# Preparing the output weights' block sums during the projections: another ring of buffers, loads 5 to 12 slots ahead, sums issued one at a time

## The chip, the cores and the metric

The kernel runs on one core of a Trainium2 chip. A core has a matrix engine (PE; its weight loads are listed as PEld), a vector engine (DVE), a scalar engine (ACT), a general-purpose engine (POOL, also called GpSimd) and a queue that issues DMA transfers (SP). Each works through its own list of instructions in order, and waits where an instruction needs what another engine or a transfer has not yet delivered. The metric is the device time of one execution in microseconds (us); lower is better.

## The reference

One layer of an encoder over two sequences (256 and 2048 rows of width 1024), in float32:

```python
h = rms_norm(x, g_pre)
proj = h @ w_in                                  # 1024 -> 3072
q, k, v, z_a, u_f, z_f = jnp.split(proj, ...)
y_a = neighbourhood_attention(q, k, v, rpb)      # 8 heads, windows of 8 x 16
y_f = fourier_mix(u_f, w_fourier, b_fourier)     # 2-D FFT by groups, then a matrix
mixed = jnp.concatenate([rms_norm(y_a, g_na) * jax.nn.silu(z_a),
                         rms_norm(y_f, g_f) * jax.nn.silu(z_f)], axis=-1)
return x + rms_norm(mixed @ w_out, g_post)
```

What matters here: `w_out` (in the code `wo`, the half of it that multiplies the Fourier branch) is used near the end of the kernel, in products of Strassen's form. Such products need differences of blocks of the weights. They depend on the weights alone, so the kernel makes them early, in a stage whose own work is the projections, and stores them in memory (`wtD`) for later.

## The kernel before

**Products.** A float32 operand is split into a high and a low part (`wa`: ACT copies the high part, L573 or L576; DVE subtracts to get the low part, L574 or L577), and each product is three matmuls (L164, L165, L166).

**The stage.** The projections to z, k and q of the long sequence run in the loop `for i in range(16)`, with an inner loop `for j in range(7)`: the seven products of a Strassen step. One pair (i, j) is a *slot*, numbered 7*i + j. A slot is 12 matmuls of 128x512 into one PSUM tile. Slots 0 to 55 work on the first half of the rows, and the change lies in these. PSUM tiles come from `mmt`, a rotation of five (three of tag `a`, two of tag `t`): the product of slot n + 5 writes the tile of slot n, so slot n must have been read out by then. Slots with j = 0 are read by ACT (L1022), all others by DVE (L935 into the output tile `f`, L1020 into a running sum).

**Order.** The order of every engine's list is that of the code: whatever is called in slot n is listed there. Engines run as far ahead or behind as their waits let them. In each slot the code calls, among others: `w_load` (weights two steps ahead) and `w_sums` (their block sums one step ahead, on POOL, L559), `a_split` (the split of the next step's weights, ACT then DVE), in some slots `n_load`, `n_scale` (DVE, L427), `n_diff` (POOL, L435, and a store `n_put`, L431) for the second half's rows, and at i = 5 `t_mask` (POOL, L612).

**The sums.** The block differences are made in four pieces x = 0 to 3, each of 128 x 1024 numbers: `wt_load` (two DMAs, L748), `wt_scale` (two ACT instructions, L754), four subtractions of 128 x 256 (L759, each depends on others of the piece), and `wt_store` (two DMAs, L765). The table `WT` gives the slot in which each step is called; within a slot these calls come after those named above, except `t_mask`. A piece lies in a tile of the pool `st` with tag `f`, three buffers in rotation. The two output tiles `o` of each step i come from the same three.

## Time and profile before

| what | value |
|---|---|
| time, median of 3 runs (lowest to highest) | 960.85 us (957.23 to 961.78) |
| the profiled execution's own time / its span | 957.96 us / 956.2 us |
| busy: PE / DVE / ACT / POOL | 944.2 / 735.0 / 505.3 / 448.2 us |
| slots 0 to 55 (first half of the projections) | 156.2 to 313.4 us of the span |

The span is the time between the first and the last instruction. PE is listed as busy for 99% of it; time that PE loses shows as gaps in its list or as a lower granted clock. In rows of the timeline a number in brackets is how long the engine sat idle before the instruction, and behind the arrow is what ended the idle time. Times of rows are counted from the start of the span.

### The profile page before, as it was taken

To read this page: it belongs to the slowest core of one execution; us is meant where nothing else is said; L and a number is where in the kernel's file an instruction comes from. 1 tells how busy PE (TensorE), PEld (TensorE's weight loads), DVE (VectorE), ACT (ScalarE), POOL (GpSimd) and SP (SyncE) were. 2 spreads that over 40 slices of the span, in tenths; PEclk is the share of its full clock that TensorE was granted. 3 is DMA by queue.
4 is the path that set the end of the run, shared out by engine and by line. 5 is a ranking of instruction groups with operands and counts; after the bars stand their busy time and mean duration, and the time that the engine had idled before them with its cause. 6 is when DMAs were issued, how large, how long until landed. Compare 5 with 4: busy or idle time off the path is not lost.

```text
span 956.2 us, 16788 instructions
## 1 busy us (share of the span) xinstructions
PE 944.2 (99%) x5595; PEld 785.2 (82%) x5595; DVE 735.0 (77%) x1355; ACT 505.3 (53%) x1085; POOL 448.2 (47%) x429
## 2 busy tenths in 40 slices
PE   9999999999899999999999999999999999999996
PEld 7889988888788888888888869877888888888885
DVE  6758987786887685598877467777688888859977
ACT  6836676423333642124344266677786676744443
POOL 4100002465770302376555236467599698624444
PEclk9999999999999999999999999999999999999999
DMA  9899697558686995489989898798998989979996
GB/s 357 298 383 335 244 341 276 174 198 323 244 330 245 357 349 192 158 310 366 301 308 365 280 341 268 216 289 265 308 282 274 279 278 305 280 262 326 318 319 218
DMA packets 148486, 276.36 MB, mean 289 GB/s; under 512 B 13126, under 2 KB 85544, under 8 KB 145648
## 3 DMA queue, kind: packets, MB, share of 16 engines
q1 hardware_dynamic: 148048, 274.88, 84.4%
q8 instruction: 45, 0.74, 0.3%
q10 hardware_dynamic: 288, 0.40, 0.1%
q14 instruction: 41, 0.34, 0.1%
q0 software_dynamic: 64, 0.02, 0.0%
HBM read 183.47 MB, written 98.90 MB: 295 GB/s over the span
## 4 chain that ended last, share of the span: by engine, by line
PE 83%; DMA 6%; DVE 5%; issue 3%; POOL 2%; ACT 1%; SPq 0%; DVEq 0%; ACTq 0%; POOLq 0%
PE mm L165 16%; PE mm L164 16%; PE mm L166 16%; PE pv L1639 6%; PE ptb L1623 6%; PE po L1550 6%; PE s L1272 4%; PE px L1706 3%; DMA yr<-yD 3%; PE pz L1706 2%; DVE of L1987 1%; DVE of L1953 1%; DMA f<-wo 1%; POOL nx L435 1%; DMA yo<-xt 1%
## 5 line engine op out<-in xcount | busy, mean ns | idle before, releaser
L164 PE MATMUL mm<-xh,wa 128*128 128x512 f32 x448 | 175.1, 391 | 2.6 <-DVE f L935 2.6
L165 PE MATMUL mm<-xl,wa 128*128 128x512 f32 x448 | 175.0, 391 | 0.0
L166 PE MATMUL mm<-xh,wa 128*128 128x512 f32 x448 | 174.9, 391 | 0.0
L559 POOL TENSOR_TENSOR ws<-wr 128x512 f32<-128x512 f32 x16 | 23.5, 1470 | 212.4 <-DMA wr<-wz 206.6
L1306 POOL TENSOR_SCALAR w<-w,m 128x465 f32<-128x465 f32 (+9 forms) x136 | 86.8, 651 | 40.3 <-DVE m L1303 21.0
L164 PEld LDWEIGHTS mm<-xh,wa 128*128 128x128 f32 x448 | 84.5, 189 | 21.2 <-issue 3.4
L166 PEld LDWEIGHTS mm<-xh,wa 128*128 128x128 f32 x448 | 84.5, 189 | 17.6
L165 PEld LDWEIGHTS mm<-xl,wa 128*128 128x128 f32 x448 | 84.4, 188 | 17.4
L574 DVE TENSOR_TENSOR wa<-wr,wa 128x512 fp32r<-128x512 f32 x60 | 73.0, 1225 | 24.1 <-ACT wa L573 24.0
L1550 PE MATMUL po<-wk,yh 128*128 128x512 f32 x280 | 86.7, 391 | 0.0
L1299 ACT ACTIVATE w<-w,m 128x465 f32<-128x465 f32 (+9 forms) x136 | 78.6, 582 | 13.9 <-DVE m L1294 13.7
L1294 DVE CUSTOM_DVE_ANT_1 w<-s,tb 128x465 f32<-128x465 f32 (+8 forms) x124 | 61.2, 531 | 10.8 <-PE s L1272 9.0
L1988 POOL TENSOR_TENSOR xt<-of,xt 128x512 f32<-128x512 f32 x34 | 43.2, 1294 | 51.9 <-issue 30.3
L612 POOL TENSOR_TENSOR mt<-mt,rmask 128x880 f32<-128x880 f32 (+2 forms) x24 | 50.3, 2111 | 32.5 <-DVE mt L608 20.4
L164 PE MATMUL mm<-vh,xh 128*128 128x512 f32 x168 | 65.4, 389 | 0.0
L165 PE MATMUL mm<-vl,xh 128*128 128x512 f32 x168 | 65.4, 389 | 0.0
L166 PE MATMUL mm<-vh,xl 128*128 128x512 f32 x168 | 65.4, 389 | 0.0
L935 DVE TENSOR_TENSOR f<-u,mm 128x512 f32<-128x512 f32 x64 | 43.5, 680 | 24.4 <-PE mm L166 17.5
L1550 PEld LDWEIGHTS po<-wk,yh 128*128 128x128 f32 x280 | 52.2, 188 | 10.9 <-issue 0.4
L1623 PE MATMUL ptb<-ident,w 128*120 128x128 f32 (+8 forms) x422 | 58.9, 277 | 0.0
L1639 PEld LDWEIGHTS pv<-pt,v 120*64 120x64 f32 (+9 forms) x880 | 47.4, 136 | 12.4 <-issue 7.3
L1623 PEld LDWEIGHTS ptb<-ident,w 128*120 128x120 f32 (+8 forms) x422 | 47.5, 140 | 12.1 <-issue 5.5
(326 smaller groups left out, 2458.9 us busy)
## 6 DMA issues: line engine op xcount, KB each, us to landing
wr<-wz SPq DMA_DIRECT2D x48, 512.0 KB
vl<-sD SPq DMA_DIRECT2D x20, 512.0 KB
xm<-xm SPq DMA_DIRECT2D x9, 1024.0 KB
oD<-ofs SPq DMA_DIRECT2D x18, 512.0 KB
of<-oD SPq DMA_DIRECT2D x18, 512.0 KB
xt<-xn SPq DMA_DIRECT2D x18, 512.0 KB
yo<-xt SPq DMA_DIRECT2D x35, 256.0 KB
yr<-yD SPq DMA_DIRECT2D x34, 256.0 KB
```

The source lines that it names most:

```text
L164: nc.tensor.matmul(out, lh, rh, start=first, stop=False)
L165: nc.tensor.matmul(out, lh, rl, start=False, stop=False)
L166: nc.tensor.matmul(out, ll, rh, start=False, stop=last)
L574: nc.vector.tensor_tensor(out=o[:, 1], in0=src, in1=o[:, 0].bitcast(F32), op=ALU.subtract)
L612: nc.gpsimd.tensor_tensor(out=o, in0=i, in1=rmask[:, m0:m0 + n].unsqueeze(2).to_broadcast([128, n, 80]), op=ALU.add)
L1294: nc.vector.tensor_tensor_reduce(out=rows(g["w"][b][:, h, :n], w), in0=rows(g["s"][2 * b + h][:, :nr * sw(w)], sw(w))[:, :, :w], in1=tv, s ...
L1299: nc.scalar.activation(w, w, AF.Exp, bias=m[:, h:h + 1], scale=-1.0, accum_out=m[:, 2 + h:3 + h])
L1306: nc.gpsimd.tensor_scalar(w, w, m[:, 4 + h:5 + h], 1.0, ALU.mult, ALU.mult)
L1550: nc.tensor.matmul(p, (d["l"] if x == 2 else d["h"])[:, c], w(n, int(x == 1), c), start=j == 0, stop=j == 11)
L1623: nc.tensor.transpose(ptb[h][:nk, j * 128:j * 128 + 128], g["w"][b][:, h, c0:c0 + nk], ident)
L1639: nc.tensor.matmul(p[hs, b], g["v"][:nk, v, hs], g["pt"][b][:nk, h, j * 128:j * 128 + 128], start=j == 0, stop=j == len(ch) - 1)
L1706: nc.tensor.matmul(p, y[:, c], b, start=first and c == i == 0, stop=c == 1 and i == 2, skip_group_check=not first)
```

## The change

The four pieces get tiles of the pool `hp` with tag `vw`, also a rotation of three buffers and of the same size. That rotation serves the row scales that `n_scale` reads (`iv`, called at slot 6, read until slot 27), and, from slot 54 on, the weights of the next stage (`vh`). The four subtractions of a piece are called one by one, each with a slot and an engine of its own. Of the 16, DVE had 8 and now has 2; POOL had 8 and now has 14. Loads stand 5 to 12 slots ahead of the scaling that reads them (before: 2 to 4).

```diff
     def wt_load(x):
         j, c = divmod(x, 2)
-        t = wot[x] = st.tile([128, 2, 2, 256], F32, tag="f", name="f", bufs=3)
+        t = wot[x] = hp.tile([128, 2, 2, 256], F32, tag="vw", name="wt", bufs=3)
...
-    def wt_sums(x, e):
+    def wt_sum(x, n, e):
         (a1, a2), (b1, b2) = [[wot[x][:, y, n] for n in range(2)] for y in range(2)]
-        for o, p, q in ((a1, a2, a1), (a2, b2, a2), (b2, b2, a1), (b1, b1, b2)):
-            e.tensor_tensor(out=o, in0=p, in1=q, op=ALU.subtract)
+        o, p, q = ((a1, a2, a1), (a2, b2, a2), (b2, b2, a1), (b1, b1, b2))[n]
+        e.tensor_tensor(out=o, in0=p, in1=q, op=ALU.subtract)
...
-    WT = ((15, wt_load, 0), (19, wt_scale, 0), (19, wt_sums, 0, nc.gpsimd), (20, wt_store, 0), (24, wt_load, 1),
-          (26, wt_scale, 1), (26, wt_sums, 1, nc.gpsimd), (27, wt_store, 1), (30, wt_load, 2), (33, wt_scale, 2),
-          (33, wt_sums, 2, nc.vector), (39, wt_store, 2), (47, wt_load, 3), (50, wt_scale, 3),
-          (51, wt_sums, 3, nc.vector), (51, wt_store, 3))
+    WT = ((9, wt_load, 0), (21, wt_scale, 0), (24, wt_sum, 0, 0, nc.gpsimd), (24, wt_sum, 0, 1, nc.gpsimd),
+          (24, wt_load, 1), (26, wt_sum, 0, 2, nc.gpsimd), (26, wt_sum, 0, 3, nc.gpsimd), (28, wt_store, 0),
+          (35, wt_scale, 1), (36, wt_sum, 1, 0, nc.vector), (36, wt_load, 2), (37, wt_sum, 1, 1, nc.gpsimd),
...
```

The rest of the new table: piece 1's other sums on POOL at slot 38, its store at 40; piece 2 loaded at 36, scaled at 41, summed at 42 (DVE), 43, 45 and 45, stored at 47; piece 3 loaded at 38, scaled at 47, summed at 48, 48, 49 and 50, stored at 51. Lines behind the table have numbers higher by 4 after the change (L935 becomes L939).

What this does to the lists, at three places. First ACT, slots 26 to 35. Here `wa` is the split of the next step's weights, `f` with itself as input (L940, L944) the SiLU of an output tile, `u` the reading of a product with j = 0. Before:

```order
L754 ACTIVATE f<-f,gmix 128x512 x2
L940 ACTIVATE f<-f 128x1024
L573 CAST wa<-wr 128x512
L940 ACTIVATE f<-f 128x1024
L573 CAST wa<-wr 128x512
L1022 COPY u_2317<-mm 128x512
L573 CAST wa<-wr 128x512
L573 CAST wa<-ws 128x512 x2
L573 CAST wa<-wr 128x512 x2
L754 ACTIVATE f<-f,gmix 128x512 x2
L573 CAST wa<-wr 128x512
```

After:

```order
L944 ACTIVATE f<-f 128x1024
L573 CAST wa<-wr 128x512
L944 ACTIVATE f<-f 128x1024
L573 CAST wa<-wr 128x512
L1026 COPY u_2309<-mm 128x512
L573 CAST wa<-wr 128x512
L573 CAST wa<-ws 128x512 x2
L573 CAST wa<-wr 128x512 x3
L576 ACTIVATE wa<-wr 128x512
L754 ACTIVATE wt<-wt,gmix 128x512 x2
```

The scalings of pieces 1 and 2 (slots 26 and 33) are gone from ahead of the SiLU and of the splits; piece 1's now stands at slot 35.

Second SP, the loads and stores of slots 24 to 36 (`xD<-nx` are the stores `n_put`, `wr<-wz` the weights two steps ahead, `mt<-tr` a table for `t_mask`). Before:

```order
L258 DMA wr<-wz 128x1024 x2
L748 DMA f<-wo 128x2x256 x2
L210 DMA zD<-f 128x1024
L765 DMA wtD<-f 256x1x256 x2
L210 DMA zD<-f 128x1024
L431 DMA xD<-nx 128x1024 x5
L748 DMA f<-wo 128x2x256 x2
L258 DMA wr<-wz 128x1024 x2
L431 DMA xD<-nx 128x1024 x2
```

After:

```order
L258 DMA wr<-wz 128x1024 x2
L748 DMA wt<-wo 128x2x256 x2
L210 DMA zD<-f 128x1024 x2
L431 DMA xD<-nx 128x1024 x3
L765 DMA wtD<-wt 256x1x256 x2
L431 DMA xD<-nx 128x1024 x2
L258 DMA wr<-wz 128x1024 x2
L431 DMA xD<-nx 128x1024 x2
L947 DMA kD<-f 128x1024 x2
L602 DMA mt<-tr 128x1200
L748 DMA wt<-wo 128x2x256 x2
```

Piece 1 is loaded in the same place, its store is no longer between the two stores of z, and the load of piece 2 has moved behind all stores `n_put` and behind the load of `mt`.

Third POOL, slots 28 to 40. Before:

```order
L435 TENSOR_TENSOR nx<-nx 128x1024 x4
L559 TENSOR_TENSOR ws<-wr 128x512
L559 TENSOR_TENSOR ws<-ws,wr 128x512
L559 TENSOR_TENSOR wr<-wr 128x512
L559 TENSOR_TENSOR wr<-wr,ws 128x512
L612 TENSOR_TENSOR mt<-mt,rmask 128x880
```

After:

```order
L435 TENSOR_TENSOR nx<-nx 128x1024 x4
L559 TENSOR_TENSOR ws<-wr 128x512
L559 TENSOR_TENSOR ws<-ws,wr 128x512
L559 TENSOR_TENSOR wr<-wr 128x512
L559 TENSOR_TENSOR wr<-wr,ws 128x512
L759 TENSOR_TENSOR wt<-wt 128x256 x3
L612 TENSOR_TENSOR mt<-mt,rmask 128x880
```

Three sums of piece 1 now stand ahead of the masks. Ahead of these rows POOL had four sums at slot 19 and four at slot 26; it now has four, those of piece 0, in slots 24 and 26. Seven further ones (pieces 2 and 3) follow in slots 43 to 50.

More of the change, by code (lines that the diff above doesn't have):

```diff
@@ L765, in wt_store @@
             nc.sync.dma_start(wtD[j, y].rearrange("p (n e) -> p n e", n=2)[:, :, 256 * c:256 * c + 256], t[:, y])
-    WT = ((15, wt_load, 0), (19, wt_scale, 0), (19, wt_sums, 0, nc.gpsimd), (20, wt_store, 0), (24, wt_load, 1),
-          (26, wt_scale, 1), (26, wt_sums, 1, nc.gpsimd), (27, wt_store, 1), (30, wt_load, 2), (33, wt_scale, 2),
-          (33, wt_sums, 2, nc.vector), (39, wt_store, 2), (47, wt_load, 3), (50, wt_scale, 3),
-          (51, wt_sums, 3, nc.vector), (51, wt_store, 3))
+    WT = ((9, wt_load, 0), (21, wt_scale, 0), (24, wt_sum, 0, 0, nc.gpsimd), (24, wt_sum, 0, 1, nc.gpsimd),
+          (24, wt_load, 1), (26, wt_sum, 0, 2, nc.gpsimd), (26, wt_sum, 0, 3, nc.gpsimd), (28, wt_store, 0),
+          (35, wt_scale, 1), (36, wt_sum, 1, 0, nc.vector), (36, wt_load, 2), (37, wt_sum, 1, 1, nc.gpsimd),
+          (38, wt_sum, 1, 2, nc.gpsimd), (38, wt_sum, 1, 3, nc.gpsimd), (38, wt_load, 3), (40, wt_store, 1),
+          (41, wt_scale, 2), (42, wt_sum, 2, 0, nc.vector), (43, wt_sum, 2, 1, nc.gpsimd),
+          (45, wt_sum, 2, 2, nc.gpsimd), (45, wt_sum, 2, 3, nc.gpsimd), (47, wt_store, 2), (47, wt_scale, 3),
+          (48, wt_sum, 3, 0, nc.gpsimd), (48, wt_sum, 3, 1, nc.gpsimd), (49, wt_sum, 3, 2, nc.gpsimd),
+          (50, wt_sum, 3, 3, nc.gpsimd), (51, wt_store, 3))
     wor = {}
```

## The prediction

> **What bounds the kernel now.** I read the page first, then the stretches of the first half of the projections, then PE's timeline at the places that stood out, then the waits there. The page says that PE is the bound, and that one of its few listed waits lies in the stage that is changed:
>
> ```profile
> PE 944.2 (99%) x5595; PEld 785.2 (82%) x5595; DVE 735.0 (77%) x1355; ACT 505.3 (53%) x1085; POOL 448.2 (47%) x429
> POOL 4100002465770302376555236467599698624444
> L164 PE MATMUL mm<-xh,wa 128*128 128x512 f32 x448 | 175.1, 391 | 2.6 <-DVE f L935 2.6
> ```
>
> In the stretches (us of the stretch; busy us and instructions of PE, PEld, DVE, ACT, POOL; granted clock; DMA share; GB/s) slots 0 to 27 run without a gap, and so does everything from 267 on:
>
> ```profile
> 156.20:232.50 76.30, 76.30 (x338) 63.07 (x337) 58.20 (x72) 32.41 (x52) 38.92 (x25) 1.00 0.67 232
> 232.50:243.40 10.90, 10.90 (x49) 8.82 (x47) 7.38 (x10) 2.80 (x4) 5.29 (x6) 1.00 0.62 231
> 243.40:260.60 17.20, 16.46 (x73) 13.44 (x72) 13.62 (x14) 6.49 (x11) 14.45 (x7) 1.00 0.68 235
> 260.60:263.70 3.10, 1.27 (x6) 0.86 (x5) 3.01 (x6) 0.15 (x2) 0.00 (x0) 0.99 0.95 341
> 263.70:267.10 3.40, 3.40 (x9) 2.67 (x8) 2.25 (x3) 1.62 (x3) 2.00 (x2) 0.50 1.02 419
> 267.10:313.40 46.30, 46.30 (x206) 38.30 (x205) 38.02 (x42) 17.52 (x22) 16.52 (x10) 1.00 0.78 280
> ```
>
> 28 slots of 12 matmuls take 76.3 us: 2.72 us a slot, 0.227 a matmul from start to start. At that rate 56 slots take 152.6 us; the six stretches hold 157.2. So 4.6 us are lost here, and PE's timeline shows where, as starts further apart than 0.227:
>
> ```profile
> 243.19 0.39 PE L166 MATMUL mm<-xh,wa 128*128 128x512 f32 x1
> 244.31 0.47 PE L164 MATMUL mm<-xh,wa 128*128 128x512 f32 x1 [0.74 <-DVE f L935]
> 244.62 0.39 PE L165 MATMUL mm<-xl,wa 128*128 128x512 f32 x1
> ...
> 260.49 0.39 PE L166 MATMUL mm<-xh,wa 128*128 128x512 f32 x1
> 262.71 0.47 PE L164 MATMUL mm<-xh,wa 128*128 128x512 f32 x1 [1.83 <-DVE f L935]
> 263.01 0.39 PE L165 MATMUL mm<-xl,wa 128*128 128x512 f32 x1
> ...
> 263.75 0.63 PE L165 MATMUL mm<-xl,wa 128*128 128x512 f32 x1
> ...
> 267.12 0.39 PE L164 MATMUL mm<-xh,wa 128*128 128x512 f32 x1
> ```
>
> Slots 32 and 38 start late because DVE has not read out the product of five slots earlier. Why DVE is late is in the rows of SP, ACT, POOL and DVE there:
>
> ```profile
> 226.34 1.55 SPq L748 DMA_DIRECT2D f<-wo  x2
> 236.99 1.34 ACT L754 ACTIVATE f<-f,gmix 128x512 f32<-128x512 f32 x2 [9.07 <-DMA f<-wo]
> 237.79 3.53 POOL L759 TENSOR_TENSOR f<-f 128x256 f32<-128x256 f32 x4 [10.30 <-ACT f L754]
> 239.82 0.90 DVE L574 TENSOR_TENSOR wa<-wr,wa 128x512 fp32r<-128x512 f32 x1 [3.52 <-ACT wa L573]
> 243.49 0.68 DVE L935 TENSOR_TENSOR f<-u,mm 128x512 f32<-128x512 f32 x1
> 249.40 10.83 POOL L435 TENSOR_TENSOR nx<-nx 128x1024 f32<-128x1024 f32 x4 [0.46 <-DMA xD<-nx]
> 255.04 1.27 SPq L748 DMA_DIRECT2D f<-wo  x2
> 258.76 1.46 ACT L754 ACTIVATE f<-f,gmix 128x512 f32<-128x512 f32 x2 [9.90 <-issue]
> 259.52 2.45 DVE L759 TENSOR_TENSOR f<-f 128x256 f32<-128x256 f32 x4 [1.56 <-ACT f L754]
> 261.88 0.68 DVE L935 TENSOR_TENSOR f<-u,mm 128x512 f32<-128x512 f32 x1
> ```
>
> First chain: piece 1 is asked for at 226.34 and scaled two slots later in ACT's list; ACT stands still for 9.07 us, with the splits of the next weights queued behind; DVE waits for the split (3.52) and reads slot 27's product only at 243.49. POOL waits 10.30 us for the same scaling. Second chain: that delays POOL's `n_diff` to 249.40, SP waits for these to store them, so piece 2 is asked for at 255.04; ACT stands still 9.90 us; DVE has piece 2's four sums ahead of a read-out, which comes at 261.88.
>
> **The change part by part.**
>
> *First stall:* 244.31 - 243.19 and 244.62 - 244.31, less 0.227 each: 0.89 + 0.08 = 0.97 us. Its cause is a load read two slots after its issue. Now 11 slots (30 us) lie between, and the list has no scaling at all between slots 21 and 35. The load took 236.99 - 226.34 = 10.65 us under the traffic there. Removed: 0.97.
>
> *Second stall:* 262.71 - 260.49 and 263.01 - 262.71, less 0.227 each: 1.99 + 0.07. Then the granted clock is 0.50 for 3.4 us: eight starts from 263.75 to 267.12 take 3.37 instead of 1.82 us, 1.55 lost. Together 3.6. Both its causes go: the wait for piece 2's load, and the DVE sums ahead of the read-out.
>
> The Trainium skill (TensorE: Matmul & The Clock Gate, What's actually happening) says that the clock falls to half after about 3.4 us of idling; by that the 1.83 us here would have cost no clock, and the sum would be 1.55 less. The row at 0.50 disagrees, and the trace decides.
>
> *Where the sums go.* Durations of a sum and of a scaling, with those of a DVE split, in ns (shortest, median, longest):
>
> ```profile
> L759 POOL TENSOR_TENSOR f<-f x8: 738/744/1069, 216.8 to 240.3; 128x256 f32<-128x256 f32 x8
> L759 DVE TENSOR_TENSOR f<-f x8: 419/426/997, 259.5 to 302.1; 128x256 f32<-128x256 f32 x8
> L754 ACT ACTIVATE f<-f,gmix x8: 708/726/727, 214.5 to 298.4; 128x512 f32<-128x512 f32 x8
> L574 DVE TENSOR_TENSOR wa<-wr,wa x30: 677/693/2287, 150.8 to 262.5; 128x512 fp32r<-128x512 f32 x30
> ```
>
> DVE loses 6 sums, 6 x 0.426 = 2.6 us; POOL gains 6 x 0.744 = 4.5 us. Seven sums stand in slots 43 to 50, some 278 to 300 us, where POOL's row on the page has a 7, then 0 (slices 11 and 12 from zero, 263 to 311 us): idle time hides them. Between slots 28 and 41 POOL has three sums; in the trace it did four there, at 237.79, so it is not fuller than before. A POOL that does not wait 10.30 us starts `n_diff` some 7 us earlier (its next wait is for DVE's scaling of those rows), and SP with it. Cost on the path: none. Were that cover gone, a late POOL would delay `w_sums`, the splits and the read-outs; the point from which PE feels it is below.
>
> *Scalings:* eight instructions of 0.726 as before, none removed. Moves only, ACT is 53% busy.
>
> *Loads and stores:* 16 issues as before, in another order. Piece 0's load, 512 KB, now stands ahead of the weights called at slot 10 instead of those of slot 17; at the 232 GB/s of that stretch it delays them by 2.3 us. They are split from slot 14 on and multiplied from slot 21 on, so that is covered. Piece 2's load stands behind all `n_put` and behind `mt`; if it lands as slowly as piece 1's did, 10.65 us or 4 slots after an issue at slots 37 to 38, ACT reaches it at slot 41 and waits for at most about a slot. A wait that is new on SP: piece 1's store (slot 40) waits for POOL's sums of slot 38. Behind it queue the stores of the masks and of k, whose tiles the read-outs of slots 43 on need; but those of the masks wait for POOL, behind the same sums, in any case. Zero.
>
> *The rings:* tag `f` serves only output tiles again, so o[1] of a step no longer waits for a store of the step before. In `vw` the buffer that piece 2 takes was last read at slot 27, and the last piece's is needed by weights called in the next stage; I find no late reader. Zero from below; from above, a wait for a store of the same size as the one listed for a load, 2 to 10 us once, of which the read-outs' slack hides all or most.
>
> *The slack:* five tiles rotate, so a read-out may end 5 x 2.72 - 2.9 = 10.7 us after its product's last matmul ends. Slot 27's product ended about 232.7 and was read out at 244.17: 11.5, hence the first stall.
>
> Sum: 0.97 + 3.6 = 4.6 us. From the profiled execution's 957.96 (span 956.2 and 1.8 around it): 953.4. Whether the gain reaches the end is told by PE's list of waits over the whole span:
>
> ```profile
> PE mm L164 <- DVE f L935: 2.6, 2, 1.8
> PE idle L251 <- POOL onesq L247: 1.0, 1, 1.0
> PE mm L170 <- DVE xl L310: 0.8, 1, 0.8
> ```
>
> The two stalls are the first row; the other two are the start of the kernel. Behind 267 PE waits for nobody, so what comes earlier there stays earlier.
>
> The profiled execution is 2.9 under the median. If runs differ by the size of these stalls (a second fall of the clock alone is 1.55), the new median is 953.4; if by something outside, 956.3. PE's list has few other gaps that could vary, but I cannot show it from one trace. I take the middle: **954.8 us**.
>
> **The rivals.**
>
> *A part of the loss stays.* For it: piece 2's load still follows the stores of POOL's results, and one scaling and one DVE sum stand at slots 35, 36, 41 and 42, just where the second stall was. Against: they read loads 5 and 11 slots old. If only the first stall goes and the second stays: 957.96 - 0.97 = 957.0, and 958.4 with half of the 2.9.
>
> *The loads are not early.* Position in a list is not time: SP in order may reach pieces 2 and 3 as late as before (the load at 255.04 was called at slot 30 and issued at slot 35), and ACT then waits at slots 41 and 47 for as long. For it: the `n_put` ahead. Against: POOL's delay came from the scaling that is gone. The loss is then only shifted: 960 us, no change.
>
> *GpSimd holds DVE up* (the slower side). The same DVE split takes 0.69 us alone and up to 2.29 beside POOL; DVE's first sum took 1.00 instead of 0.43 while POOL's `n_diff` ran. The Trainium skill (SBUF — State Buffer, SBUF: two separate sides) calls it an exclusive lock between the two, held for a whole instruction, when a DVE instruction has two SBUF inputs; the trace agrees. The place is slots 35 to 50, where ten sums join `w_sums`, the masks and the splits; each can hold DVE 0.744 us. It decides once read-outs lag by more than 10.7 us: then PE stalls at about 3.6 us a time, clock included. Three such stalls, one per step i = 5, 6, 7: 957.96 - 4.6 + 10.8 = 964.2, with half the 2.9 965.6. Against it: three sums in a step are 2.2 us, POOL is no fuller at slots 28 to 41 and idle after 287, and DVE sheds 2.6 us.
>
> **How the numbers follow.** Forecast 0.63, a part stays 0.22, loads not early 0.07, GpSimd 0.08. I count over 0.5% (4.8 us) as what a measurement can tell; faster then means under 956.05, which lies inside the forecast's own spread of 953 to 957. Of the forecast I give 0.49 to faster and 0.14 to no change; of the part that stays 0.05 and 0.17; the loads not early are no change, GpSimd is slower: faster 0.54, same 0.38, slower 0.08. Range: below, all 4.6 gone on a run like the fastest before, 957.23 - 4.6 = 952.6, less 1 for what a freer POOL and DVE may add: 951.6; above, the loss kept at the old median: 960.9.
>
> **What would show it.** PE without a wait for DVE's read-out in slots 0 to 55, no clock of 0.50 between 157 and 550, the stage at 152.6 us; ACT without idle time ahead of L754; POOL without idle time ahead of its sums; `n_diff` of slot 29 starting near 242; no longer splits than before at 278 to 300. I am wrong if a gap of PE appears at slots 38 to 50, if L754 still waits for `wt<-wo`, or if the stage is short and the time at the end is given back later.

## The result, and the profile after

The changed kernel takes 956.07 us (median of 11 executions, 953.85 to 957.37). The kernel before, timed beside it, takes 960.85 us (11 executions, 957.23 to 962.83). The ratio is 0.9953, with a 95% interval of 0.9939 to 0.9967: 0.5% faster. A second set beside the last experiments gave 956.05 against 960.14 us, ratio 0.9957 (0.9942 to 0.9972); one execution of the kernel before, of 5364 us, is left out of it. The forecast was 954.8 us, in a range from 951.6 to 960.9. The prediction's own line between faster and no change was 956.05 us; the median of the first set lies 0.02 us above it, on the border. The profiled execution took 956.58 us, with a span of 954.8.

Three lines of the page after the change: PE's wait for the read-out (`DVE f`) is gone, and another one has appeared, on a line that waited for nobody before.

```profile
PE 943.6 (99%) x5595; PEld 784.7 (82%) x5595; DVE 731.9 (77%) x1349; ACT 505.5 (53%) x1085; POOL 459.4 (48%) x435
L164 PE MATMUL mm<-xh,wa 128*128 128x512 f32 x448 | 174.4, 389 | 0.0
L165 PE MATMUL mm<-vl,xh 128*128 128x512 f32 x168 | 65.5, 390 | 1.9 <-DVE vl L505 1.9
```

DVE has six instructions less and POOL six more. `vl` is the low part of the next stage's weights, which are loaded (`op_load`) at slots 52 and 53 and split (`op_split`) at slots 54 and 55. In stretches that answer to those shown of before, with the next stage behind them:

```profile
156.20:232.50 76.30, 76.30 (x339) 63.06 (x338) 57.81 (x72) 32.63 (x52) 39.28 (x25) 1.00 0.69 233
232.50:243.40 10.90, 10.90 (x49) 8.79 (x47) 9.18 (x12) 1.57 (x3) 4.74 (x3) 1.00 0.34 127
243.40:260.60 17.20, 17.20 (x76) 14.19 (x76) 15.29 (x15) 6.75 (x12) 12.06 (x6) 1.00 0.81 301
260.60:267.10 6.50, 6.50 (x30) 5.40 (x29) 5.59 (x7) 3.19 (x6) 6.42 (x5) 1.00 1.00 364
267.10:308.90 41.80, 41.80 (x187) 34.58 (x185) 31.60 (x32) 16.20 (x20) 25.34 (x18) 1.00 0.83 306
308.90:387.20 78.30, 76.44 (x337) 62.98 (x336) 53.95 (x58) 31.02 (x32) 14.62 (x6) 1.00 0.73 275
```

The granted clock is 1.00 throughout, and PE is busy in every stretch up to 308.9. Slots 0 to 55 take 152.7 us instead of 157.2: the stage is 4.5 us shorter. The next stage takes 78.3; before, it took 76.2 us, from 313.39 to 389.55, without idle time of PE. PE's timeline at slot 32 and at the start of the next stage:

```profile
243.12 0.39 PE L166 MATMUL mm<-xh,wa 128*128 128x512 f32 x1
243.51 0.47 PE L164 MATMUL mm<-xh,wa 128*128 128x512 f32 x1
...
308.89 0.39 PE L164 MATMUL mm<-vh,xh 128*128 128x512 f32 x1
311.14 0.50 PE L165 MATMUL mm<-vl,xh 128*128 128x512 f32 x1 [1.86 <-DVE vl L505]
```

Of the first stall 0.16 us is left in front of slot 32 (0.39 from start to start instead of 0.227) and 0.07 behind its first matmul. At the next stage 2.2 us are lost.

**Why the next stage waits.** PE comes 4.5 us earlier, but what it needs does not. For each kernel (before, then after) these are DVE's `vl`, SP's last store of the sums, its loads of the weights `vr`, and the cast that reads them; for the kernel before also the first matmul that uses `vl`:

```profile
313.62 0.39 PE L165 MATMUL mm<-vl,xh 128*128 128x512 f32 x1
310.48 2.54 DVE L505 TENSOR_TENSOR vl<-vr,vh 128x1024 fp32r<-128x1024 f32 x2
301.63 1.52 SPq L765 DMA_DIRECT2D wtD<-f  x2
303.20 1.54 SPq L258 DMA_DIRECT2D vr<-wv  x2
309.39 1.06 ACT L504 CAST vh<-vr 128x1024 fp32r<-128x1024 f32 x1 [2.73 <-DMA vr<-wv]
```

```profile
309.87 2.35 DVE L505 TENSOR_TENSOR vl<-vr,vh 128x1024 fp32r<-128x1024 f32 x2
295.14 1.20 SPq L765 DMA_DIRECT2D wtD<-wt  x2
296.40 1.51 SPq L258 DMA_DIRECT2D vr<-wv  x2
307.11 1.05 ACT L504 CAST vh<-vr 128x1024 fp32r<-128x1024 f32 x1 [0.68 <-DMA vr<-wv]
```

Before, the store waited on SP for DVE's last four sums (4.2 us), and the loads of `vr` behind it were issued at 303.20 and read at 309.39: 6.2 us. Now the store does not wait, the loads are issued 6.8 us earlier, and they are read at 307.11: 10.7 us later. The stretches say why (the last two columns are the share of the DMA engines and GB/s), before and after:

```profile
290.50:296.50 6.00, 6.00 (x28) 4.99 (x27) 4.59 (x5) 0.00 (x0) 0.00 (x0) 1.00 0.29 115
296.50:302.50 6.00, 6.00 (x28) 4.96 (x27) 2.28 (x5) 2.07 (x4) 0.00 (x0) 1.00 0.88 331
302.50:308.50 6.00, 6.00 (x28) 4.97 (x27) 5.01 (x5) 3.58 (x2) 0.00 (x0) 1.00 0.92 289
```

```profile
286.00:292.00 6.00, 6.00 (x28) 4.99 (x27) 6.00 (x7) 3.04 (x4) 5.39 (x5) 1.00 0.26 87
292.00:298.00 6.00, 6.00 (x28) 4.96 (x27) 1.38 (x3) 0.59 (x1) 1.44 (x2) 1.00 0.91 328
298.00:304.00 6.00, 6.00 (x28) 4.97 (x27) 2.20 (x2) 1.91 (x1) 0.00 (x0) 1.00 0.96 339
```

The transfers for the next stage (`xl` and `vr`) are bunched behind a stretch in which the DMA engines do little (0.26), and then fill them. The first half of `vl` is therefore ready only 0.7 us earlier (309.87 plus half of 2.35, against 310.48 plus half of 2.54), with PE 4.5 us earlier. Before, PE used it at 313.62, 1.9 us after it was ready: that was all the slack there was.

**From profile to profile.** Four numbers from PE's timeline of each profile: the stage is from the first matmul of slot 0 to the first of the next stage; the next stage ends with the first matmul of the second half; the rest goes to the end of the span. With no wait of PE in them, the two take 152.5 and 76.2.

| profile | slots 0 to 55 | next stage | rest | span | median of the timed executions |
|---|---|---|---|---|---|
| before | 157.2 | 76.2 | 566.7 | 956.2 | 960.85 |
| before, second profile | 157.1 | 76.2 | 568.5 | 957.9 | - |
| after | 152.7 | 78.3 | 567.6 | 954.8 | 956.07 |
| after, second profile | 152.5 | 78.8 | 569.2 | 956.5 | 956.05 |
| third piece's sums to POOL | 155.7 | 77.4 | 568.8 | 958.0 | 958.28 |
| ring and lead alone | 159.1 | 76.3 | 569.5 | 961.1 | 961.70 |
| after, weights loaded earlier | 153.6 | 86.3 | 569.3 | 965.4 | 967.65 |
| after, loaded and split earlier | 152.5 | 76.2 | 567.6 | 952.7 | 955.85 |
| the same, second profile | 153.1 | 77.4 | 567.9 | 954.6 | 955.95 |
| after without lead | 158.0 | 77.6 | 569.4 | 961.3 | 960.78 |
| after, all sums on DVE | 152.7 | 78.0 | 567.7 | 954.6 | 958.89 |
| before without n_scale | 154.3 | 76.2 | 570.7 | 957.6 | - |
| before, n_scale spread | 162.5 | 76.2 | 571.3 | 966.2 | 966.62 |
| loaded and split earlier, n_scale spread | 152.5 | 76.2 | 568.4 | 953.2 | 955.01 |

Slot 0 starts between 156.1 and 156.5 us in all of them. The rest, which the change does not touch, differs by up to 2.5 us between the four profiles of the two kernels; among other things PE waits there for ACT (`yh`) in some executions, for 0.2 to 0.9 us, and not in others. So a single profile tells the stages to 0.1 us, but the whole only to 2 or 3.

### The profile page after: what moved, and what is told of

Its sections match the earlier page's. It is cut to its first block, busy times and chain, and to the rows that moved or that the text cites. A ratio compares the mean times of both kernels' runs of the same rounds, so it can differ in the third digit from the quotient of the medians.

```text
span 954.8 us, 16783 instructions
## 1 busy us (share of the span) xinstructions
PE 943.6 (99%) x5595; PEld 784.7 (82%) x5595; DVE 731.9 (77%) x1349; ACT 505.5 (53%) x1085; POOL 459.4 (48%) x435
## 4 chain that ended last, share of the span: by engine, by line
PE 88%; DMA 5%; DVE 4%; issue 2%; SPq 0%; ACT 0%; DVEq 0%; ACTq 0%
PE mm L165 18%; PE mm L164 18%; PE mm L166 18%; PE pv L1643 6%; PE ptb L1627 6%; PE po L1554 6%; PE s L1276 4%; PE px L1710 3%; DMA yr<-yD 2%; PE pz L1710 2%; DMA yo<-xt 2%; DVE of L1991 1%; DVE of L1957 1%; DMA xl<-xD 1%; PE py L164 1%
## 5 line engine op out<-in xcount | busy, mean ns | idle before, releaser
L574 DVE TENSOR_TENSOR wa<-wr,wa 128x512 fp32r<-128x512 f32 x60 | 69.3, 1162 | 22.1 <-ACT wa L573 21.9
L939 DVE TENSOR_TENSOR f<-u,mm 128x512 f32<-128x512 f32 x64 | 43.4, 679 | 21.4 <-PE mm L166 12.5
```

The lines of the kernel that those rows point to most:

```text
L574: nc.vector.tensor_tensor(out=o[:, 1], in0=src, in1=o[:, 0].bitcast(F32), op=ALU.subtract)
```

## The experiments

### The kernel before, a second profile

No edit.

> The kernel before once more, for a second profile. Eleven runs of it lie between 957.2 and 962.8 us, and the profiled one took 957.96, so a typical run loses about 3 us more than the profile shows. If the two stalls of slots 32 and 38 are what varies, slots 0 to 55 take more than 157.2 us here whenever the time is above 958, by about the same difference, with a second fall of the clock (1.55 us) or a longer idle time. If something else varies, the stage stays within 0.5 us of 157.2 and the difference lies at the start, in a later stage or behind the last product.

959.70 us; span 957.9. The stage loses the same 4.6 us, and the 1.7 us by which the span is longer lie in the rest (568.5 instead of 566.7). But the stage loses them in another place:

```profile
245.83 0.76 PE L164 MATMUL mm<-xh,wa 128*128 128x512 f32 x1 [2.28 <-DVE f L935]
245.63:249.04 3.41, 3.21 (x8) 2.57 (x9) 1.47 (x4) 3.33 (x6) 1.82 (x2) 0.50 0.42 169
```

Here slot 32 waits 2.28 us and the half clock (0.50 in the second row) falls on it; the wait at slot 38 is only 0.28 us. So "0.97 and 3.6" were the amounts of one execution. In both profiles PE waits 2.6 us in all and one half clock comes on top; how the wait divides over the two slots differs, for where PE is held back at slot 32 its later slots leave the read-outs more room. Two profiles do not show that the sum is always the same.

### The third piece's sums on POOL

```diff
-          (33, wt_sums, 2, nc.vector), (39, wt_store, 2), (47, wt_load, 3), (50, wt_scale, 3),
+          (33, wt_sums, 2, nc.gpsimd), (39, wt_store, 2), (47, wt_load, 3), (50, wt_scale, 3),
```

> The kernel before with one word changed: piece 2's four sums, listed at slot 33, on POOL instead of DVE; loads, scalings, ring and slots as before. Theory A (the prediction's: ACT standing still for loads asked for too late causes both stalls): ACT still stands still about 9 and 10 us, so both stalls stay, ratio 0.998 to 1.002. Theory B (the second stall came from sums that waited in DVE's list ahead of a read-out, whatever ACT did): the stall at slot 38 and its half clock are gone, some 3.6 us, ratio 0.995 to 0.997, although ACT's idle time ahead of the scaling of piece 2 stays near 10 us; the stall at slot 32 stays.

958.28 us, ratio 0.9982 (0.9971 to 0.9994).

```profile
260.01 0.72 ACT L754 ACTIVATE f<-f,gmix 128x512 f32<-128x512 f32 x1 [9.74 <-issue]
261.58 3.57 POOL L759 TENSOR_TENSOR f<-f 128x256 f32<-128x256 f32 x4
259.29 0.67 DVE L935 TENSOR_TENSOR f<-u,mm 128x512 f32<-128x512 f32 x1
265.45 0.50 PE L164 MATMUL mm<-xh,wa 128*128 128x512 f32 x1 [0.40 <-ACT u L1022]
```

ACT stands still for piece 2's load as long as before (9.74 us against 9.90), and yet of the second stall only 0.40 us and no half clock remain. The first stall stays (2.26 us of idle time in this profile), so PE waits 2.7 us in all, no less than before, and the stage is shorter (155.7 us) by about the half clock alone. That PE came later to slot 38 would by itself shrink the second stall, as in the profile above. The cause is to be read from DVE's row: the read-out of slot 33 starts at 259.29 instead of 261.88, although the read-outs ahead of it are 1.4 us later than in the first profile, and it ends with 2.2 us to spare. So that stall needs the four sums in DVE's list ahead of the read-out; ACT's wait alone does not make it. The ratio lies in the range expected of the other theory, and above that of this one: the 3.6 us were not gained.

### The ring and the lead, without the new slots

```diff
-        t = wot[x] = st.tile([128, 2, 2, 256], F32, tag="f", name="f", bufs=3)
+        t = wot[x] = hp.tile([128, 2, 2, 256], F32, tag="vw", name="wt", bufs=3)
...
-    WT = ((15, wt_load, 0), (19, wt_scale, 0), (19, wt_sums, 0, nc.gpsimd), (20, wt_store, 0), (24, wt_load, 1),
-          (26, wt_scale, 1), (26, wt_sums, 1, nc.gpsimd), (27, wt_store, 1), (30, wt_load, 2), (33, wt_scale, 2),
-          (33, wt_sums, 2, nc.vector), (39, wt_store, 2), (47, wt_load, 3), (50, wt_scale, 3),
+    WT = ((9, wt_load, 0), (19, wt_scale, 0), (19, wt_sums, 0, nc.gpsimd), (20, wt_store, 0), (16, wt_load, 1),
+          (26, wt_scale, 1), (26, wt_sums, 1, nc.gpsimd), (27, wt_store, 1), (28, wt_load, 2), (33, wt_scale, 2),
+          (33, wt_sums, 2, nc.vector), (39, wt_store, 2), (38, wt_load, 3), (50, wt_scale, 3),
```

> The kernel before with the other ring and earlier loads alone: loads called at slots 9, 16, 28 and 38, scalings, sums (two pieces on POOL, two on DVE) and stores at the old slots. Theory A: both stalls gone, ratio 0.994 to 0.997, slots 0 to 55 in about 152.7 us. Theory B: the sums on DVE no longer wait much, so the second stall shrinks to below 1 us or goes, 0.995 to 0.998; the one at slot 32, about 0.8 us, stays because DVE is behind with the scaling of rows (L427). If the sums' mere time on DVE (1.7 us) were the cause, the second stall would stay: 0.998 to 1.001.

961.70 us, ratio 1.0019 (1.0004 to 1.0034): slower, if by little. PE stalls in slots 29 to 32 four times (0.36, 0.12, 0.58 and 1.33 us) and at slot 38 for 2.83 us.

```profile
230.00 1.33 ACT L754 ACTIVATE wt<-wt,gmix 128x512 f32<-128x512 f32 x2
260.36 5.14 DVE L759 TENSOR_TENSOR wt<-wt 128x256 f32<-128x256 f32 x4
```

The scaling of piece 1 waits for no load any more, and the first stall is there all the same. It is no clean test of that wait, though: SP asks for the rows of `n_scale` 3.6 us later than before (225.85 instead of 222.26), and DVE starts on them 4.0 us later (232.67 instead of 228.65). The scaling of piece 2 still waits 4.56 us for its load, but it is over at 257.3, ahead of the sums. These four sums take 5.14 us on DVE (one of them 2.61), beside POOL's instructions; before they took 2.45. Earlier loads alone bring nothing here, which none of the three expectations had. The ring without the lead was not run.

### After, with the loads two slots ahead again

```diff
-    WT = ((9, wt_load, 0), (21, wt_scale, 0), (24, wt_sum, 0, 0, nc.gpsimd), (24, wt_sum, 0, 1, nc.gpsimd),
-          (24, wt_load, 1), (26, wt_sum, 0, 2, nc.gpsimd), (26, wt_sum, 0, 3, nc.gpsimd), (28, wt_store, 0),
-          (35, wt_scale, 1), (36, wt_sum, 1, 0, nc.vector), (36, wt_load, 2), (37, wt_sum, 1, 1, nc.gpsimd),
-          (38, wt_sum, 1, 2, nc.gpsimd), (38, wt_sum, 1, 3, nc.gpsimd), (38, wt_load, 3), (40, wt_store, 1),
+    WT = ((19, wt_load, 0), (21, wt_scale, 0), (24, wt_sum, 0, 0, nc.gpsimd), (24, wt_sum, 0, 1, nc.gpsimd),
+          (26, wt_sum, 0, 2, nc.gpsimd), (26, wt_sum, 0, 3, nc.gpsimd), (28, wt_store, 0),
+          (33, wt_load, 1), (35, wt_scale, 1), (36, wt_sum, 1, 0, nc.vector), (37, wt_sum, 1, 1, nc.gpsimd),
+          (38, wt_sum, 1, 2, nc.gpsimd), (38, wt_sum, 1, 3, nc.gpsimd), (39, wt_load, 2), (40, wt_store, 1),
```

> The changed kernel with the loads back at 2 slots ahead of the scaling (slots 19, 33, 39 and 45); ring, scalings, sums and stores as changed. Theory A (lead is what counts): ACT stands still for about 9 us at slots 21 and 35, the stalls come back, ratio 0.998 to 1.003. Theory B (what counts is that no scaling and no sum stands in slots 26 to 34, and that no read-out on DVE stands behind a sum that waits for ACT): most of the gain stays, 0.995 to 0.998, with ACT's idle time ahead of L754 back.

(The load of piece 3 moves to slot 45 in the same way.) 960.78 us, ratio 1.0013 (1.0000 to 1.0026): the whole gain is gone. The stage takes 158.0 us. PE waits 1.21 us at slot 32 (ACT waited 2.57 us for piece 0's load at slot 21, DVE behind it 3.89 us for a split, and the read-out of slot 27 ends 11.9 us after its product), and at slot 40:

```profile
267.28 1.42 ACT L754 ACTIVATE wt<-wt,gmix 128x512 f32<-128x512 f32 x2 [5.56 <-DMA wt<-wo]
268.60 0.57 ACT L1026 COPY u<-mm 128x512 f32<-128x512 f32 x1
269.22 0.80 PE L164 MATMUL mm<-xh,wa 128*128 128x512 f32 x1 [2.36 <-ACT u L1026]
```

The scaling of piece 1 waits 5.56 us for its load, the read-out of slot 35 (`u`) is listed behind it on ACT, and PE waits for that, with half a clock behind it. So the new slots alone bring nothing either. An early load is worth something because a product of slots with j = 0 is read out by ACT itself: at slot 35 a scaling that waits holds PE directly.

### After, with all sixteen sums on DVE

```diff
-          (41, wt_scale, 2), (42, wt_sum, 2, 0, nc.vector), (43, wt_sum, 2, 1, nc.gpsimd),
+          (41, wt_scale, 2), (42, wt_sum, 2, 0, nc.vector), (43, wt_sum, 2, 1, nc.vector),
```

and so on for the other thirteen; the slots stay.

> The changed kernel with all 16 sums on DVE. In the changed kernel's profile the product of slot 27 was read out 10.74 us after its end, at the limit, with DVE busy scaling rows (L427) in slots 24 to 28. If POOL matters as a place for the sums, piece 0's four sums (4 x 0.43 = 1.7 us), now on DVE at just that place, push the read-out over the limit: a stall of about 1.5 us at slot 32, with or without a fall of the clock, ratio 0.997 to 1.000. If the exclusive hold of POOL on DVE costs as much as the sums themselves do on DVE, nothing changes: 0.994 to 0.997.

958.89 us, ratio 0.9987 (0.9972 to 1.0003), with executions from 955.23 to 963.30. Against the changed kernel's 0.9953, POOL as the place of the sums is worth some 3 us of the gain. The profiled execution was one of the quickest (956.39), and its stages are those of the changed kernel, so where the slower ones lose is not shown. What its profile shows is the price of a sum: two of piece 0's take 2.94 us while POOL works, the other two 0.87 while it is idle.

```profile
235.56 2.94 DVE L759 TENSOR_TENSOR wt<-wt 128x256 f32<-128x256 f32 x2
```

### Before, without the n_scale of slots 24 to 27

```diff
-                        n_scale(x, *divmod(y - 3, 2))
+                        if x == 0:
+                            n_scale(x, *divmod(y - 3, 2))
```

> The kernel before without the scaling of rows in slots 24 to 27 (eight instructions L427 on DVE); the rows it leaves unscaled go into the sums as they are, so the values of the long sequence's second half are not those of the reference. All waits for loads of pieces 1 and 2 stay. Theory A: ACT's stand of about 9 us ahead of piece 1's scaling causes the stall at slot 32; it stays. Theory B: DVE was behind with this scaling; without it slot 27 is read out less than 9 us after its end and slot 32 starts on time, 1 to 4 us less in slots 0 to 37; the stall at slot 38 may stay.

The kernel leaves out eight of the sixteen instructions that scale the second half's rows, so its values are not the reference's. 959.42 us (one execution); the stage takes 154.3 us instead of 157.2.

```profile
237.32 1.34 ACT L754 ACTIVATE f<-f,gmix 128x512 f32<-128x512 f32 x2 [9.14 <-DMA f<-wo]
240.15 0.89 DVE L574 TENSOR_TENSOR wa<-wr,wa 128x512 fp32r<-128x512 f32 x1 [7.88 <-ACT wa L573]
240.96 0.68 DVE L935 TENSOR_TENSOR f<-u,mm 128x512 f32<-128x512 f32 x1
```

ACT waits for piece 1's load as long as before (9.14 us against 9.07), DVE now stands idle for 7.88 us behind it, and slot 27 is still read out 8.7 us after its end (240.96 + 0.68, less 232.96), inside the limit of 10.7. There is no stall at slot 32. The one at slot 38 remains (1.50 us). So ACT's wait alone does not make the first stall: it needs the eight instructions of `n_scale` in DVE's list as well.

### Before, with n_scale spread

```diff
...
-                    elif 3 <= y < 7:
+                    elif x == 0 and 3 <= y < 7:
                         n_scale(x, *divmod(y - 3, 2))
-                    elif 7 <= y < 12:
+                    elif x == 0 and 7 <= y < 12:
                         n_diff(x, y - 7)
+                    elif x == 1 and 3 <= y < 9:
+                        for z in {3: (0,), 4: (1,), 5: (2,), 6: (3,), 7: (4, 5), 8: (6, 7)}[y]:
+                            n_scale(x, *divmod(z // 2, 2), (z % 2,))
+                    elif x == 1 and 9 <= y < 14:
+                        n_diff(x, y - 9)
...
```

> The kernel before with n_scale in slots 24 to 29 (1, 1, 1, 1, 2, 2) and n_diff two slots later, nothing else. If the first stall (slot 32) comes from the wait for piece 1's load together with n_scale in DVE's list, the lag at slot 27 falls under 10.7 us and the stall goes, with ACT's wait ahead of the scaling of piece 1 still at 8 to 10 us: 1 to 2.3 us less at slot 32. If ACT's wait alone makes it, the stall stays at 1 us or more. In both cases piece 2's load, behind the stores of n_diff, comes later, and the second stall (slot 38 or 39) stays or grows to 3 to 6 us. Time: 957 to 961, ratio 0.997 to 1.002.

966.62 us, ratio 1.0066 (1.0046 to 1.0085): slower, and 5.6 us above the upper end of what was expected. The lag at slot 27 is 10.3 us and slot 32 starts in time. But the stall has moved with n_scale: slot 34 waits 2.42 us for slot 29's product, which is read out behind its last two instructions (2.41 us at 248.47). And slot 38 waits 3.73 us. Each is followed by half a clock.

```profile
253.68 10.55 POOL L435 TENSOR_TENSOR nx<-nx 128x1024 f32<-128x1024 f32 x4 [3.35 <-DMA xD<-nx]
259.34 7.98 DVE L759 TENSOR_TENSOR f<-f 128x256 f32<-128x256 f32 x4
268.07 0.47 PE L164 MATMUL mm<-xh,wa 128*128 128x512 f32 x1 [3.73 <-DVE f L935]
```

`n_diff` starts 4.3 us later than before (253.68 instead of 249.40), and the four sums of piece 2 run beside its last two instructions and the `w_sums` behind them: 7.98 us instead of 2.45, two of the sums 2.62 and 2.45 us each. That is the second stall at its largest.

### After, with the next stage's weights loaded two slots earlier

```diff
-                if j in (3, 4):
-                    op_load(j - 3)
+                if j in (1, 2):
+                    op_load(j - 1)
```

> The changed kernel with the first two weight loads of the next stage (op_load 0 and 1) called at slots 50 and 51 instead of 52 and 53, ahead of the loads of xl and of piece 3's store. In the changed kernel PE waits 1.9 us for the low part of these weights (L505) at the start of the next stage. If these loads land too late because they share the way with loads issued just ahead of them, the wait is gone: 2.0 us less than the changed kernel, ratio to the kernel before 0.992 to 0.994. If what is late is ACT's and DVE's work on xl that is listed ahead of the split, that gets no earlier and the wait stays: 0.994 to 0.997.

967.65 us, ratio 1.0082 (1.0061 to 1.0102): the wait it was to remove grew to three (0.92 us for `vh`, 3.21 and 2.85 us for `vl`).

```profile
308.76 1.98 ACT L504 CAST vh<-vr 128x1024 fp32r<-128x1024 f32 x2
313.56 0.51 PE L165 MATMUL mm<-vl,xh 128*128 128x512 f32 x1 [3.21 <-DVE vl L505]
```

The weights come earlier, but their casts are still listed behind those of `xl`, and `xl`'s transfers, which now share the DMA engines with the weights (share 1.00 from 292 to 304), land later: ACT's second cast of `xl` starts at 306.94 instead of 304.51, and that of the weights at 308.76 instead of 307.11.

### After, with the weights loaded and split two slots earlier

```diff
+                if j in (1, 2):
+                    op_load(j - 1)
...
-                    op_load(j - 3)
-                if j in (5, 6):
-                    op_split(j - 5)
+                    op_split(j - 3)
```

> The changed kernel with the next stage's first two weight loads called at slots 50 and 51 (as in e3_opload) and their splits at slots 52 and 53 instead of 54 and 55, so that ACT and DVE make them before the splits of xl. In the changed kernel PE waits 1.9 us for L505 at the start of that stage; with the loads alone earlier (e3_opload) it waited longer, because ACT stood for xl, listed ahead of the weights' split, while DMA was at its full share. Theory C (the order of this preparation is what holds PE): the wait goes, slot 56's predecessor starts without a gap, 2 us less than the changed kernel, ratio to the kernel before 0.991 to 0.994. Rival D (DMA is full there, whatever stands first is paid for by what stands behind): a wait of 1 us or more appears a few slots into the stage instead, for xl, ratio 0.994 to 0.999.

955.85 us, ratio 0.9953 (0.9936 to 0.9969). With the order of the casts changed too, the wait is gone in this profile (297.26 instead of 307.11 for the first cast), and the span of 952.7 is 2.1 us shorter than that of the changed kernel:

```profile
297.26 1.05 ACT L504 CAST vh<-vr 128x1024 fp32r<-128x1024 f32 x1 [3.89 <-DMA vr<-wv]
309.13 0.39 PE L165 MATMUL mm<-vl,xh 128*128 128x512 f32 x1
```

The median, however, is only 0.2 us lower, and so the two were timed again, side by side.

### The changed kernel and this one again

No edit to either.

> The changed kernel once more, with a second profile. If the wait of 1.86 us for the low part of vl (DVE, L505) at the start of the next stage belongs to the kernel, it stands in this profile too, between 1 and 3 us, and the stage of slots 0 to 55 again has no stall over 0.3 us. If it is chance, PE passes from slot 55 into the next stage without a wait, and the span is near 952.5. Time: 956 +- 0.7 us, ratio 0.994 to 0.997, either way.

> The changed kernel with the next stage's weights loaded at slots 50 and 51 and split at slots 52 and 53, once more, beside the changed kernel on the same chip. If the wait for vl costs the changed kernel 2 us in most executions, this one is 1 to 2 us faster than the changed kernel: 954.0 to 955.0, ratio 0.992 to 0.994. If the wait is there in few executions, or if what comes earlier here is lost again behind, the two agree within 0.5 us.

956.05 us, ratio 0.9957 (0.9942 to 0.9972), and 955.95 us, ratio 0.9949 (0.9930 to 0.9969): no difference that can be told, within the 0.5 us expected for that case. The changed kernel shows its wait for `vl` again, at 2.33 us. The other kernel has none for `vl`, but in this execution 0.30 us at slot 32 and 0.96 us some 5 us into the next stage, where a read-out on DVE (L1024) is late instead. The wait for `vl` is a property of the changed kernel; that removing it would gain its 2 us is not confirmed.

### This one with n_scale spread

The edit of n_scale above, on the kernel with the weights loaded and split earlier.

> The same as the one before, and the eight instructions of n_scale for the second half's rows, two in each of slots 24 to 27, stand in slots 24 to 29 as 1, 1, 1, 1, 2, 2, with n_diff two slots later. If what still varies between executions of the changed kernel is the lag of DVE's read-outs behind n_scale (10.74 us at slot 27, the limit), the lag there falls below 9 us and the median by 0.5 to 1.5 us: 953.5 to 955. If the variation lies elsewhere (at the end, where PE waits for the last branch's operands), the median stays within 0.5 us of the kernel before this one. If the later n_diff makes the stores and the masks late, PE stalls at slots 38 to 45 and the time is over 957.

955.01 us (954.23 to 957.03), ratio 0.9947 (0.9929 to 0.9966). The lag of the read-out of slot 27 behind its product falls to 6.0 us (10.7 and 10.3 in the two profiles of the changed kernel, 9.3 and 11.0 in those of the kernel above), the largest between slots 0 and 52 is 7.7, and PE has no wait in the stage, nor in the next:

```profile
156.10:308.60 152.50, 152.50 (x675) 126.17 (x673) 122.49 (x136) 62.24 (x91) 87.95 (x54) 1.00 0.75 266
308.60:384.80 76.20, 76.20 (x338) 63.12 (x337) 49.97 (x56) 28.43 (x30) 15.12 (x6) 1.00 0.73 271
```

Its median is the lowest of all kernels here, 1.0 us under that of the changed kernel, but the intervals overlap, and the two cannot be told apart. The edit that makes the kernel before 6 us slower costs nothing here: `n_diff` starts at 248.11, no later than in the changed kernel (248.55), and behind it a single sum (1.51 us), not a block of four, stands in DVE's list.

## Why the prediction was right, point by point

**What bounds the kernel, and the size of the loss: right.** The 4.6 us between 157.2 and 152.6 were predicted to go, and 4.5 did (152.7, and 152.5 in the second profile). No clock of 0.50 is left in the stage, ACT does not wait ahead of the scaling of piece 1 (259.67) and 0.83 us ahead of that of piece 2, where it had waited 9.07 and 9.90 us, and POOL does not wait ahead of the sums of piece 0. (ACT does stand still for 9.21 us shortly ahead of piece 1's scaling, but for the weights `wr`, which the split listed there reads.)

**First stall: the size right, the cause half right.** "Its cause is a load read two slots after its issue" leaves out the other half. Without n_scale the same wait of ACT, 9.14 us, stalls nobody. With the wait gone and n_scale 4.0 us later, in the kernel with ring and lead alone, PE stalls all the same. In the changed kernel DVE is as far behind as it may be:

```profile
239.14 1.06 ACT L944 ACTIVATE f<-f 128x1024 f32<-128x1024 f32 x1 [11.29 <-DVE f L939]
234.99 3.47 DVE L427 SCALAR_TENSOR_TENSOR nx<-nx,gpre,iv 128x512 f32<-128x512 f32 x2
242.68 0.68 DVE L939 TENSOR_TENSOR f<-u,mm 128x512 f32<-128x512 f32 x1
```

Slot 27 is read out 0.81 us earlier than before (243.36 instead of 244.17), with a lag of 10.7 us: exactly the limit. ACT stands still as long as ever, only now it waits for DVE, whose n_scale takes 3.47 us for two instructions beside POOL's `w_sums`, and 2.37 for two beside POOL's sums of piece 0 (1.40 and 1.41 while POOL is idle). The first stall went with ACT's wait, but there was nothing to spare: in the changed kernel with weights split earlier, slot 32 waits 0.30 us in one of two profiles.

**Second stall: the size right, one of the two causes not needed.** "The wait for piece 2's load, and the DVE sums ahead of the read-out" were both held responsible. Moving the sums to POOL with the wait left as it was removed all but 0.4 us of it; moving the load and leaving the sums left 2.83 us, with DVE not waiting ahead of them. In the kernel before the wait added 1.56 us of idle time on DVE, but the sums are what the stall cannot do without. What the prediction did not see is that the wait returns as a cause of its own once the scaling stands ahead of ACT's read-out at slot 35: that is what the lead is needed for (2.36 us at slot 40 without it). The change needs both lead and slots; each without the other gave 1.0019 and 1.0013, and both with all sums on DVE 0.9987.

**Where the sums go: right in what PE pays, wrong in POOL's time and in one step.** POOL is busy for 11.2 us longer (459.4 instead of 448.2), not 4.5: its sums take 1.12 us at the median and up to 2.67, where the prediction had 0.744. They cost PE nothing all the same, and the splits on DVE between 278 and 300 are hardly longer than before (L577: 1215 and 1188 ns on average, 1168 and 1184 before). "A POOL that does not wait 10.30 us starts n_diff some 7 us earlier", near 242, was wrong:

```profile
246.84 1.30 POOL L559 TENSOR_TENSOR wr<-wr,ws 128x512 f32<-128x512 f32 x1 [7.22 <-DVE wa L574]
248.55 10.82 POOL L435 TENSOR_TENSOR nx<-nx 128x1024 f32<-128x1024 f32 x4 [0.41 <-DMA xD<-nx]
```

It started at 248.55, 0.85 us earlier: POOL waited 7.22 us for a split on DVE instead. The prediction had named another one, and no length ("its next wait is for DVE's scaling of those rows"): that scaling was over at 242.76, and the split that `w_sums` needs came only at 246.00.

**The rings and the loads: right.** No engine waits for a store of the sums; SP does twice, for 0.3 and 0.4 us. With piece 0's load ahead of other weights the read-out of slot 13 lags by 7.3 and 8.1 us in the two profiles, before by 5.6 and 6.7, inside the limit; that the load is the reason is not shown, since the last kernel above has the same load and a lag of 5.7.

**"What comes earlier there stays earlier": wrong.** It rested on a list of waits in which the next stage waited for nobody. That list holds no slack, and the slack was 1.9 us for a gain of 4.5. The wait for `vl` gave back 2.2 us in the first profile and 2.6 in the second. The text named this as a way to be wrong, "the time at the end is given back later", but priced it at nothing. That what holds PE there is the order of the preparation is shown by the kernel with the weights loaded and split earlier, which has no wait for `vl` in two profiles. In the sum: 956.2 - 4.4 for the stage + 2.2 for the next + 0.9 in the rest (567.6 less 566.7) = 954.9, the measured span but for rounding.

**The median.** The forecast took half of the 2.9 us between profile and median as caused by the stalls. The profile before was quick in the rest as well (566.7 us; the other profiles of all kernels have 567.6 to 571.3), so some of the difference lay outside the change. At the end of the next stage the profiles of after stand 2.1 to 2.3 us ahead of those of before (387.2 and 387.4 against 389.6 and 389.5 us), while the medians differ by 4.8 and 4.1. The other half of the gain is therefore in executions that no profile caught; whether the kernel before has both stalls at once with half a clock in each, more often than these two profiles show, stays open. So it is in part luck that the median lies within 1.3 us of the forecast: the next stage took back about half of the 4.6 us, and about as much came from where no profile shows it.

**The rivals.** "A part of the loss stays" names a stall that is not there; a part of the gain was lost, but at the start of the next stage. "The loads are not early" fell: the lead is early enough and needed. "GpSimd holds DVE up" made no stall at slots 35 to 50 (DVE's two sums took 1.51 us each instead of 0.43), but its mechanism has a share in the second stall of the kernel before: beside `n_diff` three splits on DVE take 1.69 to 2.33 us (0.69 while POOL is idle), and the first of the four sums 1.00 instead of 0.43. In the kernel with n_scale spread it cost more than it was priced at: 3.73 us of idle time and a half clock.

## What to carry to other kernels

Before a gain in one stage is booked at the end, look up for the first instructions of the next stage when their operands were ready, not only whether they waited: a list of waits shows no slack, and here 1.9 us of it left, in the profiles, 2.2 us of a gain of 4.5. (The median did not follow when the wait was removed.) When an engine in order falls behind, write down everything in its list over the last limit's length (here 10.7 us) and not only the wait in front of the late instruction; a stall that has two causes can go when one is removed, and come back when the other grows. A block of elementwise work on DVE is priced by what GpSimd runs beside it: the same four sums took 1.87 us with GpSimd idle (piece 3 before, at 300.65), 2.45 with the first of them beside it, and 5.14 and 7.98 us with more of them beside it.

## What was unexpected in the hardware

The granted clock falls to 0.50 for 3.4 us after some short idle times of PE and not after others of the same length. It fell after 1.83 us (before, slot 38), 2.28 (the second profile of before), 2.36 (after without lead), 2.42 and 3.73 us (before with n_scale spread); it did not after 1.86 and 2.33 us (both profiles of after, next stage), 2.26 (sums to POOL) and 2.83 us (ring and lead alone). So the length of one idle time does not decide. The Trainium skill (TensorE: Matmul & The Clock Gate, What's actually happening) says that activity is judged in windows of about 3.4 us that run freely. The traces agree: in each profile all changes of the granted clock, from its rise at the start of the kernel to its last fall, lie whole multiples of 3.413 us apart. In the kernel before with n_scale spread, for example, two falls lie five windows apart:

```profile
252.34:255.76 3.42, 3.42 (x9) 2.63 (x8) 3.42 (x4) 0.00 (x0) 2.08 (x1) 0.50 1.05 381
269.41:272.82 3.41, 3.41 (x10) 2.64 (x9) 3.41 (x6) 0.35 (x1) 1.28 (x1) 0.50 1.05 378
```

The borders of the windows can therefore be laid through each profile (before, one lies at 263.66, where the clock falls; after, with no fall in these stages, they follow from the clock's rise at 6.47 us). Counting in each window what PE's starts lost against one every 0.227 us, the two stages of all 14 profiles give one picture: behind every window with 1.99 us or more the clock is 0.50 for the next window, and behind none with 1.89 or less. The wait of 1.86 us after the change was cut by a border at 310.26, into windows that lost 1.14 and 0.88; the 1.83 us before, with 1.99 lost from start to start, fell into one. In the kernel with the weights loaded earlier the half clock lasted three windows, 10.24 us, because PE lost 2.3 and 2.5 us in the first two of them. For an estimate of a stall's price this means: nothing more below about 2 us, and above it 0 or 1.6 us more, depending on where a border falls, which differs from execution to execution.

One load shows how little the issue time says when the DMA engines are full: the weights `vr` were issued 6.8 us earlier and could be read 2.3 us earlier (10.7 instead of 6.2 us from issue to the cast).
